# S5 parameters with both exponents on VectorE, and weight chunks in alternating order

## The chip, the cores and the metric

The kernel runs on one core of one Trainium2 chip. The metric is the device time of one execution in microseconds (us); lower is better. Engines are named TensorE (PE, its weight loads PEld), VectorE (DVE), ScalarE (ACT), GpSimd (POOL) and SyncE (SP, which issues most DMAs).

## The reference

One layer of a hybrid decoder trunk in float32, with 256 positions and a width of 2048:

```python
h = rmsnorm(x, norm1_w)
proj = h @ w_in                      # retention q,k,v,gate; mLSTM qk,v,o,gates; S5 input u
mix = concat[ silu(r_g) * groupnorm(retention(rope(q), rope(k), v)),     # 6 heads
              sigmoid(m_o) * groupnorm(mlstm(conv_silu(m_qk), m_v, gates)),  # 6 heads
              s5(u) ]                                                    # 32 groups, 64 states
x = x + mix @ w_out
h = rmsnorm(x, norm2_w)
x = x + (silu(gate) * val) @ w_down  # val, gate = split(conv3(h @ w_up)), 5632 each
return rmsnorm(x, final_norm_w)
```

The S5 part first turns its parameters, 32 groups of 64 complex states, into a discrete system:

```python
step = exp(log_step)[:, None]
mag = exp(ar * step)
abar_re, abar_im = mag * cos(ai * step), mag * sin(ai * step)
xr, xi = abar_re - 1.0, abar_im
den = ar * ar + ai * ai
fr, fi = (xr * ar + xi * ai) / den, (xi * ar - xr * ai) / den
```

It then scans the state over the 256 positions, reads it out, applies a gelu and a gated linear unit (GLU).

## The kernel before, in words

**Products.** Every float32 weight chunk of up to 1024 columns is loaded into a raw buffer (wr, 4 of them), cast by ScalarE to a high half (wh, 4), and VectorE writes the remainder as a low half (wl, 3). Activations are kept as a pair, high half beside low half, 256 columns each. `fm_tile` (line 521) computes one feature-major tile of 128 outputs: per chunk of eight blocks, `fm_part` (line 512) first runs eight matmuls of wh against the pair (512 columns, the high pass), then eight of wl against the high half (256 columns, the low pass), all into one PSUM bank. `chunk` (line 422) asks, at the start of each chunk, for loads five ahead, casts three ahead and remainders two ahead.

**Order of the work.** The S5 input product comes first (a loop over k at line 1200, with four or eight matmuls of each half per step), then 6 tiles for rotary queries and keys, 2 token-major tiles, 12 tiles of the mLSTM convolution, 6 token-major tiles, the output projection (partly as parts of chunks, with the GLU between, and 10 whole tiles), then 88 up tiles, 14 down tiles of 44 blocks (six chunks), and a token-major end.

**The planner.** Up to the MLP each engine's order is written out while the program is built. Every wrapped instruction (`V`, `S`, `G`, `mm`) advances a model clock of its engine by an estimated cost. Side work is a list of generators; `pump` (line 270) resumes one when the time that it yielded is due on VectorE's model clock and that clock isn't more than 0.35 us ahead of TensorE's. `hi_tasks` (evacuations, convolutions) go first, then `lo_tasks` in the order in which they were added: retention heads, gates, mLSTM heads, S5 parameters, S5 inputs, the four S5 groups, gelu. In the MLP a scheduler orders the engines by program order.

**S5 parameters.** `s5_params` (line 583) runs on POOL on tiles of 128 x 16: `exp_` (line 445) of the log step, the angle, its reduction and two series, `exp_` for the magnitude, three squarings of (cos, sin), the denominator with a power of -1, the two factors, and seven more squarings for the table of turns. POOL's `scalar_tensor_tensor` (line 221) is two POOL instructions. After POOL, VectorE multiplies the input matrices with the factors, TensorE transposes them, and VectorE doubles tables of cosine and sine out to 128 positions (line 686). `s5_inputs` and `s5_group` (lines 723 and 744) then take two PSUM banks and a pair of banks for each of the four groups, and VectorE does two pairs per group: products with the tables, scans, products back; 32 small matmuls read the state out.

**The start.** In the loop at line 1200, step j waits for its load of x and weights; ScalarE writes the high half of the activations, VectorE the low half (`xs[k][:, T:]`) and wl, and TensorE's matmuls read both.

Of the kernel before, what the change touches and what calls it, by code (L numbers as in the profile page):

```python
# [40 lines left out]
def kernel(ctx: ExitStack, tc: tile.TileContext, a: dict, out: bass.AP):  # L41
# [189 lines left out]
    def mm(o, lhsT, rhs, start, stop, par=1):  # L231
        fast = lhsT.dtype == F32R
        c = max(free(o) / 2400.0, 0.107) * (1 if fast else 4 if free(o) > 64 else 2) / par
        run("pe", c, [o], [lhsT, rhs])
        nc.tensor.matmul(o, lhsT=lhsT, rhs=rhs, start=start, stop=stop)  # L235
# [206 lines left out]
            "p (a b) -> p a b", a=shape[1]) if len(shape) > 2 else neg_half[:, :shape[1]], op=ALU.pow)  # L442
        return z

    def exp_(x, shape, lo=-87.0, hi=88.0):

        c, n, f, p = [tp(shape) for _ in range(4)]
        ni = tp(shape, I32)
        G.tensor_scalar(c, x, lo, hi, op0=MAX, op1=ALU.min)
        G.tensor_scalar(n, c, 1.4426950408889634, 12582912.0, op0=MUL, op1=ADD)  # L450
        G.tensor_scalar(n, n, 1.0, -12582912.0, op0=MUL, op1=ADD)
        G.scalar_tensor_tensor(f, n, -0.693145751953125, c, op0=MUL, op1=ADD)
        G.scalar_tensor_tensor(f, n, -1.42860682030941723e-6, f, op0=MUL, op1=ADD)

        G.tensor_scalar(ni, n, 127.0, 8388608.0, op0=ADD, op1=MUL)
        G.tensor_scalar(p, f, 1 / 5040, None, op0=MUL)
        for k in (1 / 720, 1 / 120, 1 / 24, 1 / 6, 0.5, 1.0):
            G.scalar_tensor_tensor(p, p, k, f, op0=ADD, op1=MUL)
        r = tn(shape)
        G.scalar_tensor_tensor(r, p, 1.0, ni.bitcast(F32), op0=ADD, op1=MUL)  # L460
        return r


# [45 lines left out]
        V.scalar_tensor_tensor(dst[:, T:], src, scale, dst[:, :T], op0=MUL, op1=SUB)  # L509


    def fm_part(ps, hl, ks, k0, acts, nk):

        h, l = hl
        ws = [(k, slice((k - k0) * 128, (k - k0 + 1) * 128)) for k in ks]
        for k, w in ws:
            mm(ps, lhsT=h[:, w], rhs=acts[k], start=(k == 0), stop=False)
        for k, w in ws:
            mm(ps[:, T:], lhsT=l[:, w], rhs=acts[k][:, :T], start=False, stop=(k == nk - 1))

    def fm_tile(first, acts, nk=KT):
        ps = acc_t()
        per = CH // 128
        for c in range(0, nk, per):
            fm_part(ps, chunk(first + c // per), range(c, min(c + per, nk)), c, acts, nk)
            if not auto[0]:
                pump()
        return ps
# [50 lines left out]
    def keep_up():  # L579

        return "dve", clk.pool

    def s5_params():
        sh = [128, 16]
        step_ = exp_(P("ls"), sh)
        yield keep_up()
        arg, th = tn(sh), tn(sh)
        G.tensor_tensor(arg, P("are"), step_, op=MUL)
        G.tensor_tensor(th, P("aim"), step_, op=MUL)

        c2 = math.floor((2.0 * math.pi - 6.28125) * 2.0 ** 20) / 2.0 ** 20
        c3 = 2.0 * math.pi - 6.28125 - c2
        k, ph, z, s, v, t = [tn(sh) for _ in range(6)]
# [9 lines left out]
        for cs, cc in ((1 / 120, -1 / 720), (-1 / 6, 1 / 24), (None, -0.5)):  # L603
# [4 lines left out]
        G.scalar_tensor_tensor(s, s, 1.0, ph, op0=ADD, op1=MUL)  # L608
        G.tensor_scalar(v, v, 1.0, 1.0, op0=MUL, op1=ADD)
        yield keep_up()  # L610
        mag = exp_(arg, sh)
        yield keep_up()

        def square(v, s):

            t, v2, s2_ = tp(sh), tn(sh), tn(sh)
            G.tensor_tensor(t, s, s, op=MUL)
            G.scalar_tensor_tensor(s2_, s, 2.0, v, op0=MUL, op1=MUL)
            G.tensor_scalar(v2, t, -2.0, 1.0, op0=MUL, op1=ADD)
            return v2, s2_  # L620

        for _ in range(3):
            v, s = square(v, s)
            yield keep_up()
        ar, ai = P("are"), P("aim")
        xr_, xi_, den, t1, t2, fr, fi = [tn(sh) for _ in range(7)]
        G.tensor_tensor(xr_, mag, v, op=MUL)
        G.tensor_tensor(xi_, mag, s, op=MUL)
        G.tensor_tensor(den, ar, ar, op=MUL)
        G.tensor_tensor(t1, ai, ai, op=MUL)  # L630
        G.tensor_tensor(den, den, t1, op=ADD)
        G.tensor_scalar(xr_, xr_, 1.0, -1.0, op0=MUL, op1=ADD)
        G.tensor_tensor(den, den, neg_one, op=ALU.pow)
        yield keep_up()
# [6 lines left out]
        turn = {1: (v, s)}  # L641
        for m in (1, 2, 4, 8, 16, 32, 64):
            turn[2 * m] = square(*turn[m])
            yield keep_up()

        yield "obj", lambda: "raws" in st
# [67 lines left out]
        st.update(cr=cr, nci=ci, ncr=ncr, ct=ct, sn=sn, er=turn[128][0], ei=turn[128][1], mag=mag)  # L714

    u_sb, y_sb = {}, {}

# [442 lines left out]
    add(ret_heads())  # L1160
    add(gates())
    add(ml_heads())
    add(s5_params())
    add(s5_inputs())
    for c in range(4):
        add(s5_group(c))
# [21 lines left out]
    clk.dve = clk.pool = 3.3  # L1188
    clk.act = 2.6
    sqs = []  # L1190

    def square():
# [4 lines left out]
            V.tensor_tensor(sqs[0], sqs[0], sq, op=ADD)  # L1197
        sqs.append(sq)

    for j, ks in enumerate(kts):  # L1200
        pump(until=max(last(raw[j].tensor.name), xat[ks[-1]]))
        if j > 1:
            highs_to(j)
        for k in ks:
            d = s2(F32R)
            S.activation(d[:, :T], xr[k // 2][:, (k % 2) * T:(k % 2 + 1) * T], AF.Copy, scale=P("n1", k))
            xs.append(d)
        if j > 1:
# [369 lines left out]
```

## Time and profile before

| what | us |
|---|---|
| median of 3 runs | 1159.4 (1158.87 to 1159.93) |
| profiled execution | 1158.52 |
| its span, first to last instruction | 1156.5 |
| TensorE busy | 1140.5 (99%) |
| VectorE busy | 870.0 (75%) |
| ScalarE busy | 625.0 (54%) |
| POOL busy | 95.0 (8%) |

Busy time is the union of an engine's instructions. Matmuls overlap in the records, so the pace of TensorE is read from the starts of successive matmuls, not from their durations. A row of the timeline merges neighbours of the same kind and gives the start of the first, the time from there to the end of the last, and their count; in brackets stand the idle time of the engine before it and what ended it.

### The profile page before, as it was taken

The numbers are of one execution on the slowest core, as the hardware profiler recorded it, in microseconds if no ns is written. First come the engines' busy times: TensorE is split into PE (matmuls) and PEld (weight loads), VectorE is DVE, ScalarE is ACT, GpSimd is POOL, SyncE is SP. The second block draws the span as 40 slices with busy tenths as digits, with TensorE's granted clock in tenths as the row PEclk, the third lists the DMA queues.
The fourth block names the chain that finished last, engine by engine and source line by source line (L and its number), as shares of the span: only waits on it lengthen the run. The fifth ranks groups of instructions, "written<-read, shape, count | busy, mean of one in ns | idle before, by whom it ended". The sixth has DMA issues, their size and how long they took to land.

```text
span 1156.5 us, 18142 instructions
## 1 busy us (share of the span) xinstructions
PE 1140.5 (99%) x6738; PEld 1013.0 (88%) x6738; DVE 870.0 (75%) x1478; ACT 625.0 (54%) x983; POOL 95.0 (8%) x228
## 2 busy tenths in 40 slices
PE   8999999999999999999999999999999999999997
PEld 7899888999778888888888888888888888888897
DVE  7778999989988678787877878778777655554554
ACT  7665555555546555555555555555555444444441
POOL 7936003010000000000000000000000000000000
PEclk9999999999999999999999999999999999999999
DMA  8667654455546656556555655656556666666662
GB/s 313 212 172 230 201 150 130 137 150 165 183 156 235 196 178 190 189 186 189 191 187 187 190 187 192 186 188 192 186 189 192 177 194 185 186 189 191 190 193 108
DMA packets 66905, 215.21 MB, mean 186 GB/s; under 512 B 7552, under 2 KB 9600, under 8 KB 66816
## 3 DMA queue, kind: packets, MB, share of 16 engines
q1 hardware_dynamic: 66672, 214.01, 59.5%
q8 instruction: 52, 0.85, 0.3%
q14 instruction: 37, 0.30, 0.1%
q10 hardware_dynamic: 144, 0.04, 0.0%
HBM read 211.92 MB, written 2.10 MB: 185 GB/s over the span
## 4 chain that ended last, share of the span: by engine, by line
PE 95%; DVE 3%; issue 1%; DMA 1%; SPq 0%; ACT 0%; POOL 0%; POOLq 0%; DVEq 0%; ACTq 0%
PE acc L235 90%; PE mis L235 3%; DVE s L183 2%; DVE wl L183 1%; PE wo L235 1%; PE u L235 1%; DMA s<-in_wu_dram 1%; PE mis L239 0%; SPq L1150 0%; SPq L385 0%; POOL t L218 0%; ACT wh L193 0%; ACT s L202 0%; DVE tp L183 0%; POOLq L1574 0%
## 5 line engine op out<-in xcount | busy, mean ns | idle before, releaser
L183 DVE TENSOR_TENSOR wl<-wr,wh 128x1024 fp32r<-128x1024 f32 (+3 forms) x409 | 473.4, 1158 | 247.8 <-PE acc L235 219.8
L193 ACT CAST wh<-wr 128x1024 fp32r<-128x1024 f32 (+3 forms) x409 | 406.4, 996 | 383.6 <-PE acc L235 338.0
L235 PE MATMUL acc<-s,wh 128*128 128x512 f32 x2372 | 602.5, 393 | 4.3 <-DVE s L183 4.3
L235 PEld LDWEIGHTS acc<-s,wh 128*128 128x128 f32 x2372 | 425.5, 189 | 81.3 <-DVE s L183 6.5
L235 PEld LDWEIGHTS acc<-s,wl 128*128 128x128 f32 x2372 | 327.4, 190 | 24.8
L235 PE MATMUL acc<-s,wl 128*128 128x256 f32 x2372 | 336.4, 282 | 0.0
L235 PE MATMUL acc<-wh,s 128*128 128x384 f32 (+2 forms) x632 | 159.4, 330 | 0.0
L183 DVE SCALAR_TENSOR_TENSOR s<-s,pp,s 128x255 f32<-128x255 f32 (+3 forms) x244 | 116.2, 479 | 3.9 <-ACT s L202 0.8
L183 DVE TENSOR_TENSOR s<-s,s 128x256 f32<-128x256 f32 (+4 forms) x242 | 111.2, 474 | 7.3 <-ACT s L202 3.2
L235 PEld LDWEIGHTS acc<-wh,s 128*128 128x128 f32 x632 | 112.2, 189 | 2.3 <-issue 1.1
L235 PE MATMUL acc<-wl,s 128*128 128x384 f32 (+2 forms) x316 | 103.0, 326 | 0.0
L202 ACT ACTIVATE s<-s,pp 128x256 f32<-128x256 f32 (+1 forms) x146 | 82.3, 567 | 16.4 <-DVE s L183 15.3
L218 POOL TENSOR_TENSOR t<-t,neg_half 128x2 f32<-128x2 f32 (+1 forms) x4 | 2.5, 632 | 892.2 <-DVE t L183 892.2
L202 ACT ACTIVATE s<-s 128x256 f32<-128x256 f32 (+2 forms) x106 | 45.5, 431 | 41.6 <-DVE s L183 41.4
L183 DVE TENSOR_TENSOR s<-acc,s 128x256 f32<-128x256 f32 x138 | 57.3, 417 | 3.5 <-PE acc L235 3.2
L235 PEld LDWEIGHTS acc<-wl,s 128*128 128x128 f32 x316 | 59.7, 189 | 0.0
L193 ACT COPY s<-acc 128x256 f32<-128x256 f32 x136 | 49.2, 364 | 12.7 <-PE acc L235 12.3
L235 PE MATMUL acc<-g,wh 128*128 128x512 f32 x196 | 50.0, 394 | 0.0
L183 DVE TENSOR_TENSOR s<-s,rbc 128x256 f32<-128x256 f32 x106 | 44.5, 423 | 3.8 <-ACT rbc L193 0.9
L235 PEld LDWEIGHTS acc<-g,wh 128*128 128x128 f32 x196 | 34.8, 188 | 6.2
L235 PE MATMUL mis<-s,s 128*32 128x256 f32 (+6 forms) x280 | 31.2, 352 | 0.6 <-DVE s L183 0.6
L235 PEld LDWEIGHTS acc<-g,wl 128*128 128x128 f32 x196 | 27.1, 189 | 2.3
(112 smaller groups left out, 487.2 us busy)
## 6 DMA issues: line engine op xcount, KB each, us to landing
wr<-in_wup_dram SPq DMA_DIRECT2D x176, 512.0 KB, 4.7
wr<-in_wdn_dram SPq DMA_DIRECT2D x70, 512.0 KB, 3.7
wr<-in_wtm_dram SPq DMA_DIRECT2D x56, 384.0 KB, 3.3
wr<-in_wfm_dram SPq DMA_DIRECT2D x36, 512.0 KB, 4.7
wr<-in_wout_dram SPq DMA_DIRECT2D x26, 512.0 KB, 4.0
wr<-in_wdt_dram SPq DMA_DIRECT2D x11, 512.0 KB, 3.8
s<-in_x_dram SPq DMA_DIRECT2D x14, 256.0 KB, 5.5
wr<-in_wdn_dram SPq DMA_DIRECT2D x14, 256.0 KB, 2.7
```

The costliest lines, as they stand in the source:

```text
L183: return real(o, *args, **kw)
L193: return nc.scalar.copy(o, i)
L202: return nc.scalar.activation(o, i, fn, **kw)
L218: return real(o, *args, **kw)
L235: nc.tensor.matmul(o, lhsT=lhsT, rhs=rhs, start=start, stop=stop)
```

## The change

`exp_` becomes a generator of steps that can run on POOL or on VectorE (with tiles of its own there). Both S5 exponents and the product between them, 29 instructions, go to VectorE: `fill` puts 3 of them ahead of each of the first two steps of the loop at line 1200 and 4 behind the activations' low halves, then 6 ahead of each later step until they are used up. The denominator and its power become POOL's first work on the parameters. `s5_params` waits until the step size has been issued, and, after three squarings, until the magnitude has. Sine and cosine lie side by side in one tile, and a squaring is three POOL instructions instead of four. The model clocks of VectorE and POOL start at 3.3 us before the S5 task is added instead of after. And `fm_tile` runs its odd chunks low pass first. The parts of the output projection, the GLU and the token-major tiles keep their order.

```diff
-    def exp_(x, shape, lo=-87.0, hi=88.0):
-        c, n, f, p = [tp(shape) for _ in range(4)]
-        ni = tp(shape, I32)
-        G.tensor_scalar(c, x, lo, hi, op0=MAX, op1=ALU.min)
...
+    def exp_steps(E, r, x, shape, lo=-87.0, hi=88.0):
+        c, n, f, p = [tn(shape) if E is V else tp(shape) for _ in range(4)]
+        ni = tn(shape, I32) if E is V else tp(shape, I32)
+        yield E.tensor_scalar(c, x, lo, hi, op0=MAX, op1=ALU.min)
...
+    def exp_(x, shape):
         r = tn(shape)
+        for _ in exp_steps(G, r, x, shape):
+            pass
         return r
...
-    def fm_part(ps, hl, ks, k0, acts, nk):
+    def fm_part(ps, hl, ks, k0, acts, nk, swap=False):
...
+        def highs():
+            for k, w in ws:
+                mm(ps, lhsT=h[:, w], rhs=acts[k], start=(k == 0), stop=(swap and k == nk - 1))
+        def lows():
+            for k, w in ws:
+                mm(ps[:, T:], lhsT=l[:, w], rhs=acts[k][:, :T], start=False, stop=(not swap and k == nk - 1))
+        for part in (lows, highs) if swap else (highs, lows):
+            part()
...
-            fm_part(ps, chunk(first + c // per), range(c, min(c + per, nk)), c, acts, nk)
+            fm_part(ps, chunk(first + c // per), range(c, min(c + per, nk)), c, acts, nk, swap=bool(c // per % 2))
...
+    def s5_exps():
+        step_, arg, mag = [tn(sh5) for _ in range(3)]
+        yield from exp_steps(V, step_, P("ls"), sh5)
+        st["step"] = step_
+        yield V.tensor_tensor(arg, P("are"), step_, op=MUL)
+        yield from exp_steps(V, mag, arg, sh5)
+        st["mag"] = mag
+    def s5_den():
...
+        G.tensor_tensor(den, den, neg_one, op=ALU.pow)
+        return den
-    def s5_params():
-        step_ = exp_(P("ls"), sh)
+    def s5_params(den):
+        yield "obj", lambda: "step" in st
...
-        mag = exp_(arg, sh)
...
+        def square(vs):
+            w, o = tp([128, 2, 16]), tn([128, 2, 16])
+            G.tensor_tensor(w, vs, vs[:, 1:2].to_broadcast([128, 2, 16]), op=MUL)
+            G.tensor_scalar(o[:, 0], w[:, 1], -2.0, 1.0, op0=MUL, op1=ADD)
+            G.tensor_scalar(o[:, 1], w[:, 0], 2.0, None, op0=MUL)
+            return o
...
+        yield "obj", lambda: "mag" in st
...
-    add(s5_params())
+    clk.dve = clk.pool = 3.3
+    add(s5_params(s5_den()))
...
+    exps = s5_exps()
+    def fill(n):
+        for _ in range(n):
+            next(exps, None)
     for j, ks in enumerate(kts):
+        fill(3 if j < 2 else 6)
         pump(until=max(last(raw[j].tensor.name), xat[ks[-1]]))
...
             V.scalar_tensor_tensor(xs[k][:, T:], xr[k // 2][:, (k % 2) * T:(k % 2 + 1) * T], P("n1", k),
                                    xs[k][:, :T], op0=MUL, op1=SUB)
+        fill(4 if j < 2 else 0)
         lows_to(j)
```

## Rows read from the trace of the kernel before

**Rows 1.** The page's summary line of the engines (busy us, share of the span, instructions) and the first line of the chain that ended last (share of the span by engine).

```profile
PE 1140.5 (99%) x6738; PEld 1013.0 (88%) x6738; DVE 870.0 (75%) x1478; ACT 625.0 (54%) x983; POOL 95.0 (8%) x228
...
PE 95%; DVE 3%; issue 1%; DMA 1%; SPq 0%; ACT 0%; POOL 0%; POOLq 0%; DVEq 0%; ACTq 0%
```

**Rows 2.** Busy time by stretch: from and to in us, length, then busy us and count of each engine, the granted TensorE clock, the busy share of the DMA engines, and GB/s.

```profile
3.10:14.00 10.90, 8.45 (x42) 7.24 (x41) 6.31 (x12) 7.07 (x13) 8.69 (x27) 1.00 0.97 341
30.00:120.00 90.00, 90.00 (x527) 82.93 (x526) 71.55 (x153) 54.77 (x94) 54.06 (x128) 1.00 0.67 209
120.00:225.00 105.00, 103.83 (x653) 93.67 (x651) 101.53 (x213) 57.09 (x98) 11.63 (x32) 1.00 0.53 155
300.00:345.00 45.00, 41.52 (x263) 31.86 (x263) 40.03 (x77) 24.44 (x41) 0.00 (x0) 1.00 0.46 149
345.00:1146.00 801.00, 800.78 (x4666) 707.68 (x4665) 561.21 (x841) 425.59 (x649) 1.24 (x2) 1.00 0.60 187
```

**Rows 3.** TensorE's timeline: the starts of two chunks of up tiles 70 chunks apart; inside one chunk the first and the sixth high matmul and the first low matmul; and two low matmuls of the token-major end, 51 matmuls of 256 columns apart.

```profile
699.39 2.00 PE L235 MATMUL acc<-s,wh 128*128 128x512 f32 x8
...
894.93 2.00 PE L235 MATMUL acc<-s,wh 128*128 128x512 f32 x8
...
704.98 0.40 PE L235 MATMUL acc<-s,wh 128*128 128x512 f32 x1
...
706.14 0.39 PE L235 MATMUL acc<-s,wh 128*128 128x512 f32 x1
...
706.82 0.28 PE L235 MATMUL acc<-s,wl 128*128 128x256 f32 x1
...
1117.00 0.28 PE L235 MATMUL acc<-wl,g 128*128 128x256 f32 x1
...
1123.12 0.28 PE L235 MATMUL acc<-wl,g 128*128 128x256 f32 x1
```

**Rows 4.** Timeline of VectorE and of TensorE: a remainder (wl) and the first matmul that reads it, in a conv tile and in an up tile.

```profile
123.86 1.22 DVE L183 TENSOR_TENSOR wl<-wr,wh 128x1024 fp32r<-128x1024 f32 x1
...
128.91 0.28 PE L235 MATMUL acc<-s,wl 128*128 128x256 f32 x1
...
702.39 1.23 DVE L183 TENSOR_TENSOR wl<-wr,wh 128x1024 fp32r<-128x1024 f32 x1 [0.77 <-PE acc L235]
...
709.62 0.28 PE L235 MATMUL acc<-s,wl 128*128 128x256 f32 x1
```

**Rows 5.** VectorE's timeline around 247 us: two small operations in the mLSTM heads, of which the second reads the first.

```profile
247.32 0.17 DVE L183 TENSOR_TENSOR t<-t,t 128x12 f32<-128x12 f32 x1
247.52 0.23 DVE L183 RECIPROCAL t<-t 128x12 f32<-128x12 f32 x1
```

**Rows 6.** VectorE's timeline at the start: its first operation, behind the landing of the parameters, and the low halves of the activations of two blocks.

```profile
3.17 0.17 DVE L183 TENSOR_SCALAR t<-pp 128x4 f32<-128x4 f32 x1 [3.17 <-DMA pp<-in_pp_dram]
...
13.51 0.87 DVE L183 SCALAR_TENSOR_TENSOR s<-s,pp,s 128x256 fp32r<-128x256 f32 x2
```

**Rows 7.** TensorE's timeline at the start: the two high passes that wait.

```profile
9.50 0.73 PE L235 MATMUL acc<-s,wh 128*128 128x512 f32 x2 [0.99 <-DVE s L183]
...
14.04 0.73 PE L235 MATMUL acc<-s,wh 128*128 128x512 f32 x2 [1.50 <-DVE s L183]
```

**Rows 8.** POOL's timeline: the two products behind the first exponent, the first instruction of the second exponent, the root of the first norm right behind its last, the denominator's power, and the first and the last of the 28 instructions of the seven squarings for the table of turns.

```profile
12.10 0.41 POOL L218 TENSOR_TENSOR t<-pp,t 128x16 f32<-128x16 f32 x2
...
28.70 1.14 POOL L218 TENSOR_SCALAR tp<-t 128x16 f32<-128x16 f32 x1
...
39.85 0.73 POOL L218 TENSOR_TENSOR t<-t,neg_half 128x2 f32<-128x2 f32 x1
...
47.70 3.09 POOL L218 TENSOR_TENSOR t<-t,neg_one 128x16 f32<-128x16 f32 x1
...
56.84 0.21 POOL L218 TENSOR_TENSOR tp<-t 128x16 f32<-128x16 f32 x1
...
66.15 0.93 POOL L218 TENSOR_SCALAR t<-tp 128x16 f32<-128x16 f32 x1
```

**Rows 9.** VectorE's timeline: the first products with the S5 factors, the first products of the first S5 group, and the first ones of the second pair of the last group.

```profile
73.25 1.28 DVE L183 TENSOR_TENSOR s<-s,t 128x512 f32<-128x512 f32 x2
...
143.50 1.28 DVE L183 TENSOR_TENSOR s<-mis,s 128x512 f32<-128x512 f32 x2
...
314.90 1.21 DVE L183 TENSOR_TENSOR s<-pj,s 128x1024 f32<-128x1024 f32 x1
```

**Rows 10.** TensorE's timeline from 300 us: the 32 read-out matmuls of the third S5 group, two waiting matmuls of the output projection, the 32 read-out matmuls of the last group in two rows, and a waiting matmul of the GLU.

```profile
300.44 1.93 PE L235 MATMUL mis<-s,s 128*32 128x256 f32 x32 [0.19 <-DVE s L183]
...
316.56 0.50 PE L235 MATMUL acc<-s,wh 128*128 128x512 f32 x1 [0.61 <-DVE s L183]
318.08 0.50 PE L235 MATMUL acc<-s,wh 128*128 128x512 f32 x1 [1.02 <-DVE s L183]
...
325.98 0.63 PE L235 MATMUL mis<-s,s 128*32 128x256 f32 x4
327.06 3.29 PE L235 MATMUL mis<-s,s 128*32 128x256 f32 x28 [0.45 <-DVE s L183]
...
332.27 0.51 PE L235 MATMUL mis<-s,wh 128*128 128x512 f32 x1 [1.03 <-DVE s L183]
```

**Rows 11.** VectorE's timeline inside POOL's power of 47.70 us.

```profile
49.29 1.75 DVE L183 TENSOR_TENSOR s<-s,s 128x256 f32<-128x256 f32 x5
```

More of the change, by code (lines that the diff above doesn't have):

```diff
@@ L443, in rsqrt_ @@
         return z
-    def exp_(x, shape, lo=-87.0, hi=88.0):
-        c, n, f, p = [tp(shape) for _ in range(4)]
-        ni = tp(shape, I32)
-        G.tensor_scalar(c, x, lo, hi, op0=MAX, op1=ALU.min)
[L450 to L456, printed above, removed]
+    def exp_steps(E, r, x, shape, lo=-87.0, hi=88.0):
+        c, n, f, p = [tn(shape) if E is V else tp(shape) for _ in range(4)]
+        ni = tn(shape, I32) if E is V else tp(shape, I32)
+        yield E.tensor_scalar(c, x, lo, hi, op0=MAX, op1=ALU.min)
+        yield E.tensor_scalar(n, c, 1.4426950408889634, 12582912.0, op0=MUL, op1=ADD)
+        yield E.tensor_scalar(n, n, 1.0, -12582912.0, op0=MUL, op1=ADD)
+        yield E.scalar_tensor_tensor(f, n, -0.693145751953125, c, op0=MUL, op1=ADD)
+        yield E.scalar_tensor_tensor(f, n, -1.42860682030941723e-6, f, op0=MUL, op1=ADD)
+        yield E.tensor_scalar(ni, n, 127.0, 8388608.0, op0=ADD, op1=MUL)
+        yield E.tensor_scalar(p, f, 1 / 5040, None, op0=MUL)
         for k in (1 / 720, 1 / 120, 1 / 24, 1 / 6, 0.5, 1.0):
-            G.scalar_tensor_tensor(p, p, k, f, op0=ADD, op1=MUL)
+            yield E.scalar_tensor_tensor(p, p, k, f, op0=ADD, op1=MUL)
+        yield E.scalar_tensor_tensor(r, p, 1.0, ni.bitcast(F32), op0=ADD, op1=MUL)
+    def exp_(x, shape):
         r = tn(shape)
-        G.scalar_tensor_tensor(r, p, 1.0, ni.bitcast(F32), op0=ADD, op1=MUL)
+        for _ in exp_steps(G, r, x, shape):
+            pass
         return r
@@ L509, in split_scaled @@
         V.scalar_tensor_tensor(dst[:, T:], src, scale, dst[:, :T], op0=MUL, op1=SUB)
-    def fm_part(ps, hl, ks, k0, acts, nk):
+    def fm_part(ps, hl, ks, k0, acts, nk, swap=False):
         h, l = hl
         ws = [(k, slice((k - k0) * 128, (k - k0 + 1) * 128)) for k in ks]
[L516 to L519, printed above, removed]
+        def highs():
[6 more added lines that the diff above has]
+            part()
     def fm_tile(first, acts, nk=KT):
@@ L581, in keep_up @@
         return "dve", clk.pool
-    def s5_params():
-        sh = [128, 16]
-        step_ = exp_(P("ls"), sh)
[L586 to L589, printed above, removed]
+    sh5 = [128, 16]
+    def s5_exps():
[6 more added lines that the diff above has]
+    def s5_den():
+        ar, ai = P("are"), P("aim")
+        den, t1 = [tn(sh5) for _ in range(2)]
+        G.tensor_tensor(den, ar, ar, op=MUL)
+        G.tensor_tensor(t1, ai, ai, op=MUL)
+        G.tensor_tensor(den, den, t1, op=ADD)
+        G.tensor_tensor(den, den, neg_one, op=ALU.pow)
+        return den
+    def s5_params(den):
+        sh = sh5
+        yield "obj", lambda: "step" in st
+        th = tn(sh)
+        G.tensor_tensor(th, P("aim"), st["step"], op=MUL)
         c2 = math.floor((2.0 * math.pi - 6.28125) * 2.0 ** 20) / 2.0 ** 20
         c3 = 2.0 * math.pi - 6.28125 - c2
-        k, ph, z, s, v, t = [tn(sh) for _ in range(6)]
+        k, ph, z, s, v = [tn(sh) for _ in range(5)]
         G.tensor_scalar(k, th, 1.0 / (2.0 * math.pi), 12582912.0, op0=MUL, op1=ADD)
@@ L607, in s5_params @@
             yield keep_up()
-        G.scalar_tensor_tensor(s, s, 1.0, ph, op0=ADD, op1=MUL)
-        G.tensor_scalar(v, v, 1.0, 1.0, op0=MUL, op1=ADD)
+        vs = tn([128, 2, 16])
+        G.scalar_tensor_tensor(vs[:, 1], s, 1.0, ph, op0=ADD, op1=MUL)
+        G.tensor_scalar(vs[:, 0], v, 1.0, 1.0, op0=MUL, op1=ADD)
         yield keep_up()
-        mag = exp_(arg, sh)
[L612 to L620, printed above, removed]
+        def square(vs):
[4 more added lines that the diff above has]
+            return o
         for _ in range(3):
-            v, s = square(v, s)
+            vs = square(vs)
             yield keep_up()
+        v, s = vs[:, 0], vs[:, 1]
+        yield "obj", lambda: "mag" in st
+        mag = st["mag"]
         ar, ai = P("are"), P("aim")
-        xr_, xi_, den, t1, t2, fr, fi = [tn(sh) for _ in range(7)]
+        xr_, xi_, t1, t2, fr, fi = [tn(sh) for _ in range(6)]
         G.tensor_tensor(xr_, mag, v, op=MUL)
         G.tensor_tensor(xi_, mag, s, op=MUL)
-        G.tensor_tensor(den, ar, ar, op=MUL)
-        G.tensor_tensor(t1, ai, ai, op=MUL)
-        G.tensor_tensor(den, den, t1, op=ADD)
         G.tensor_scalar(xr_, xr_, 1.0, -1.0, op0=MUL, op1=ADD)
-        G.tensor_tensor(den, den, neg_one, op=ALU.pow)
-        yield keep_up()
         for o, x0, x1_, op in ((fr, xr_, xi_, ADD), (fi, xi_, xr_, SUB)):
@@ L640, in s5_params @@
             yield keep_up()
-        turn = {1: (v, s)}
+        turn = {}
         for m in (1, 2, 4, 8, 16, 32, 64):
-            turn[2 * m] = square(*turn[m])
+            vs = square(vs)
+            turn[2 * m] = vs[:, 0], vs[:, 1]
             yield keep_up()
@@ L713, in s5_params @@
                 yield from double(ct[c], sn[c], slice(4 * c, 4 * c + 4), 4, m)
-        st.update(cr=cr, nci=ci, ncr=ncr, ct=ct, sn=sn, er=turn[128][0], ei=turn[128][1], mag=mag)
+        st.update(cr=cr, nci=ci, ncr=ncr, ct=ct, sn=sn, er=turn[128][0], ei=turn[128][1])
     u_sb, y_sb = {}, {}
@@ L1187 @@
     ups += [pair[:, :512], pair[:, 512:]]
-    clk.dve = clk.pool = 3.3
     clk.act = 2.6
```

## The prediction, made before the changed kernel was run

> **What bounds the kernel now.** I read the engine summary first, then the chain that ended last, then a table of stretches. TensorE is busy 1140.5 of 1156.5 us, and it is 95% of the chain [rows 1]. So only two things pay: less time per matmul, and fewer holes in TensorE's row. The table of stretches shows the holes [rows 2]: 2.45 us between 3.1 and 14.0 us, 1.17 us between 120 and 225 us, 3.48 us between 300 and 345 us, none between 30 and 120 us, and 0.22 us in the 801 us of the gated MLP. The granted clock is 1.00, the level of 2.4 GHz, in all of them. In the same table VectorE idles 18.45 us between 30 and 120 us and only 3.47 us between 120 and 225 us.
>
> **Part 1: the chunks alternate.** A chunk of a feature-major tile is eight matmuls of 512 columns (high pass), then eight of 256 (low pass). From 699.39 to 894.93 us there are 70 chunks, 2.7934 us each [rows 3]. Inside one, the first five high matmuls take 1.16 us (704.98 to 706.14), 0.232 us each, the last three 0.68 us (706.14 to 706.82), 0.2267 us each. So after a low pass TensorE needs five matmuls to come to its pace, and they cost 1.16 - 5 x 0.2267 = 0.0265 us. Matmuls of 256 columns hold 0.120 us over a long run: 51 of them from 1117.00 to 1123.12 us [rows 3]. A chunk at both steady paces would be 8 x 0.2267 + 8 x 0.120 = 2.7736 us, so one return to the high pass, with the small credit on entering the low pass, costs 2.7934 - 2.7736 = 0.0198 us.
>
> With odd chunks low pass first, the order is high, low, low, high, and the next tile begins high: every second return goes. That is one for each of the 28 feature-major tiles before the MLP (6 + 12 + 10) and the 88 up tiles, and three for each of the 14 down tiles of six chunks: 158 x 0.0198 = **3.1 us less**. The ends are 0 (the loss doubles after a doubled low pass) and 4.2 (158 x 0.0265, the credit stays). I take 3.1, since the low pace is flat after its second matmul and the high pace after its fifth. A loss is excluded: it would need a pace worse than the steady ones that the rows show.
>
> The price is that an odd chunk's low half (wl) is due a high pass, 1.84 us, earlier. In the MLP wl ends at 702.39 + 1.23 = 703.62 us and is first read at 709.62 us: 6.0 us to spare. The tightest odd chunk of the conv tiles ends at 125.08 us and is read at 128.91 us: 3.8 us [rows 4]. Both cover it. An odd chunk's wh is released a low pass later; ScalarE casts three chunks ahead of TensorE, which hides that 0.95 us; without this cover each odd chunk would cost it. No DMA moves.
>
> **Part 2: both exponents on VectorE at the start.** 29 small operations (14, one product, 14), each reading the one before. The trace has no such chain, so I bound the step from the nearest rows: dependent operations on 12 columns begin 0.20 us apart (247.32 to 247.52), and one lasts 0.17 us [rows 5]; a 4-column one during POOL's work lasts 0.17 us too [rows 6]. So 29 x 0.20 = 5.8 us. Between 3.1 and 14.0 us VectorE is busy 6.31 of 10.9 us [rows 2], so 4.6 us are free, but split into pieces by waits for ScalarE's casts. TensorE waits here: 0.99 us before 9.50 and 1.50 us before 14.04 [rows 7], both for a low half of the activations, and the second is written from 13.51 us [rows 6]. I walked the new order, 3 + 4 operations in each of the first two steps, then 6, 6 and 3. Step one and two stay covered (their matmuls wait for the casts). The 9.50 becomes about 10.5 and the 14.04 about 14.9. **0.9 us more**, on the path because TensorE has no hole afterwards until 180 us. The ends are 0 (steps of 0.16 us fit the free time) and 2 (steps of 0.24 us).
>
> **Part 3: what POOL is rid of.** The second exponent held POOL from 28.70 to 39.9 us, 11.2 us [rows 8]. The phase began at 12.10 us, behind the first exponent; now it can start when VectorE has done its first fourteen operations, near 7.5 us: 4.6 us sooner. The denominator's power takes 3.09 us [rows 8] and moves to POOL's first microseconds after the parameters land, where it ends before 7.5 us. Seven squarings of four instructions took 10.2 us (56.84 to 67.08) [rows 8], 0.37 us an instruction; ten squarings lose one each, 3.7 us, less for the double width of another: I take 3. In all POOL ends 4.6 + 11.2 + 3.1 + 3 = 22 us sooner, at about 45 us. Behind the new wait for the step size on POOL's queue stands only S5 work and the first norm's root, which waited behind the second exponent before (39.85) [rows 8].
>
> None of this is on TensorE's path by itself. VectorE began S5's products at 73.25 us and the first group at 143.50 us [rows 9]; it was then full, so groups ran late, and the last one's products (314.90) stood in front of work that TensorE waited for. With the tables some 22 us sooner, VectorE does them in its idle time before 120 us, and the groups move up by what is recovered: I take half of the 18.45 us, about 9. What is late at the end: TensorE waits 1.02 us before 318.08; the last group's 32 read-out matmuls take from 325.98 to 330.35, 4.37 us, where the third group's took 1.93 us, so 2.4 us are lost; 1.03 us go before 332.27, and about 0.4 of the 0.61 us before 316.56 [rows 10]. Together 4.9 us, the upper end; 0 is the lower. The last group's second pair starts at 314.90 us [rows 9] and its read-out ends 15 us later, so nine microseconds free most but not all of it: **3.0 us less**. What is late next are the retention and mLSTM heads' transposes, which wait for the last gate tile.
>
> **Sum.** 0.9 - 3.1 - 3.0 = -5.2 us. The profiled execution took 1158.52 us (span 1156.5, 2.0 us around it), 0.9 us under the median of 1159.4. So 1153.3 on its scale, **1154.2 us** on the median's. About 0.2% (2.3 us) can be told from no change.
>
> **The rivals.** First, the order of the passes is worth nothing: a matmul costs its columns and a constant. TensorE then keeps 2.79 us a chunk and the time is 1157.3 us. Against it, equal matmuls take 0.232 and 0.2267 us by their place [rows 3]. The Trainium skill, TensorE: Matmul & The Clock Gate, section Back-to-back issue gap, has this rule, the spacing being columns over 2.4 GHz plus 2.5 ns; the trace disagrees, with 0.2267 us and more for 512 columns.
>
> Second, S5 gains nothing: the groups' places are set by PSUM banks and by the planner, which runs heads first, or POOL does not end sooner. 0.9 - 3.1 gives 1157.2 us. For it: between 300 and 345 us VectorE idles 5.0 us while TensorE waits for it [rows 2], so its load alone does not set the order.
>
> Third, POOL's power stops VectorE at the start. The price is its 3.09 us [rows 8], so 1157.3 us. Against it, VectorE did five two-input products in 1.75 us from 49.29 us, inside the power of 47.70 to 50.79 us [rows 8, 11]. The Trainium skill, SBUF — State Buffer, section Who interferes with whom, says that such operations and a POOL read lock each other out for a whole instruction; here the trace disagrees.
>
> Fourth, slower: between 102 and 171 us, where the conv tiles leave VectorE 3.47 us in 105 [rows 2], S5 groups pulled forward fill its queue ahead of wl. It decides once VectorE falls behind by the 3.8 us margin [rows 4] less the 1.84 us: then each of the 12 odd chunks waits. At half a microsecond each, 6 us, with no gain from S5: 1159.4 + 0.9 - 3.1 + 6 = 1163.2 us.
>
> **Chances.** Forecast 0.55, first rival 0.12, second 0.18, third 0.04, fourth 0.11. The first three rivals lie at the bound of 1157.1 us, so under half of their 0.34 counts as faster: 0.52 + 0.15 = 0.67 faster, 0.21 the same, 0.12 slower. The range goes from 1150.8 (4.9 from S5, 4.2 from the order, 0.5 at the start) to 1158.4, over the three rivals with a worse start; slower is left out.
>
> **What would show it.** Right: two chunks in the MLP take 5.567 us, not 5.587; the second stall at the start ends near 14.9 us; POOL's parameters end near 45 us; the last read-out takes about 2 us. Wrong: high matmuls at 0.232 us in the second half of the run of sixteen, a first S5 product that still comes at 70 us, or holes with wl as releaser between 102 and 171 us.

## The result, and the profile after

The changed kernel takes **1148.74 us** (1148.46 to 1148.82, four runs) against 1159.13 us (1158.62 to 1159.93, four runs) before: a ratio of 0.9909, interval 0.9892 to 0.9926. That is 10.4 us less, where 5.2 were forecast, and below the range. The two profiled executions, from which the rows come, lie 9.7 us apart (1158.52 and 1148.82).

The profiled execution after: the engine summary and the chain, for [rows 1].

```profile
PE 1134.9 (99%) x6738; PEld 1012.7 (88%) x6738; DVE 867.7 (76%) x1507; ACT 625.9 (55%) x983; POOL 76.5 (7%) x171
...
PE 94%; POOL 3%; DVE 2%; issue 1%; DMA 0%; ACT 0%; POOLq 0%; DVEq 0%; SPq 0%
```

The stretches of [rows 2] after (the same columns).

```profile
3.10:14.00 10.90, 8.66 (x42) 6.64 (x41) 10.10 (x41) 7.05 (x13) 9.28 (x19) 1.00 0.97 342
30.00:120.00 90.00, 89.77 (x527) 82.37 (x526) 80.95 (x181) 54.08 (x92) 31.50 (x80) 1.00 0.67 209
120.00:225.00 105.00, 104.32 (x661) 93.62 (x661) 102.53 (x212) 58.19 (x100) 13.30 (x31) 1.00 0.51 153
300.00:345.00 45.00, 45.00 (x280) 38.69 (x279) 33.97 (x59) 26.30 (x42) 0.00 (x0) 1.00 0.63 210
```

VectorE works 80.95 of the 90 us from 30 to 120 us, up from 71.55. Between 300 and 345 us the roles have changed: TensorE has no hole, VectorE idles 11 us. The 3% of POOL in the chain are its work on the S5 parameters up to 36 us, behind which the first norm's root stands on its queue (35.94 us, before 39.85); TensorE waits 0.22 us for that norm.

POOL's timeline after, for [rows 8]: the denominator's power, the first work on the step size (0.17 us behind VectorE), the last factors, and the end of the last squaring.

```profile
4.05 3.00 POOL L218 TENSOR_TENSOR t<-t,neg_one 128x16 f32<-128x16 f32 x1
7.22 0.60 POOL L218 TENSOR_TENSOR t<-pp,t 128x16 f32<-128x16 f32 x1 [0.17 <-DVE t L183]
...
31.14 1.45 POOL L218 TENSOR_TENSOR t<-t,t 128x16 f32<-128x16 f32 x2
...
42.11 1.44 POOL L218 TENSOR_SCALAR t<-tp 128x16 f32<-128x16 f32 x2
```

VectorE's S5 work after, for [rows 9].

```profile
43.97 1.29 DVE L183 TENSOR_TENSOR s<-s,t 128x512 f32<-128x512 f32 x2
...
104.33 1.27 DVE L183 TENSOR_TENSOR s<-mis,s 128x512 f32<-128x512 f32 x2
...
290.10 1.22 DVE L183 TENSOR_TENSOR s<-pj,s 128x1024 f32<-128x1024 f32 x1
```

POOL's tables end at 43.5 us instead of 67. The first products come 29 us sooner, the first group 39 us, the last group's second pair 25 us.

TensorE after, for [rows 10]: the start of the output projection, the last group's read-out, and the matmul behind the GLU.

```profile
302.36 0.39 PE L235 MATMUL acc<-s,wh 128*128 128x512 f32 x1
...
314.25 1.93 PE L235 MATMUL mis<-s,s 128*32 128x256 f32 x32
...
330.22 0.40 PE L235 MATMUL wo<-s,wh 128*128 128x512 f32 x1
```

The same first and last matmul before.

```profile
302.50 0.48 PE L235 MATMUL acc<-s,wh 128*128 128x512 f32 x1
...
337.30 0.40 PE L235 MATMUL wo<-s,wh 128*128 128x512 f32 x1
```

Nearly the same work (182 matmuls; before, 184, with two small transposes more) takes 27.9 us instead of 34.8. The waits of [rows 10], one of 0.16 us more and the longer read-out account for some 5.2 us of the 6.9 that are gone. Of the other 1.7, the two transposes are 0.3; the rest is time lost around each wait that no idle column shows. The matmul ahead of 316.56 us, for one, starts at 315.55 us; the next would have started 0.23 us later and starts 1.01 us later, but since the record of the first lasts 0.40 us the row marks 0.61 us of these 0.78.

TensorE in the up tiles after, for [rows 3]: one period of two chunks, between two high passes 35 periods apart.

```profile
689.35 0.86 PE L235 MATMUL acc<-s,wh 128*128 128x512 f32 x3
...
706.05 3.82 PE L235 MATMUL acc<-s,wh 128*128 128x512 f32 x16
709.70 2.08 PE L235 MATMUL acc<-s,wl 128*128 128x256 f32 x16
...
884.18 1.09 PE L235 MATMUL acc<-s,wh 128*128 128x512 f32 x4
```

Two chunks take 194.83 / 35 = 5.567 us. The start, for [rows 7]: TensorE's three waits.

```profile
10.01 0.73 PE L235 MATMUL acc<-s,wh 128*128 128x512 f32 x2 [1.48 <-DVE s L183]
12.05 0.74 PE L235 MATMUL acc<-s,wh 128*128 128x512 f32 x2 [0.38 <-DVE s L183]
14.11 0.73 PE L235 MATMUL acc<-s,wh 128*128 128x512 f32 x2 [0.37 <-DVE s L183]
```

And for [rows 6], VectorE's low half for the last of them.

```profile
13.57 0.88 DVE L183 SCALAR_TENSOR_TENSOR s<-s,pp,s 128x256 fp32r<-128x256 f32 x2
```

Where the time went, from the start of each part's first matmul, with the two halves of the change run apart (below):

| first matmul of | before | after | order alone | S5 alone |
|---|---|---|---|---|
| rotary tiles | 30.95 | 31.02 | 31.25 | 31.08 |
| ten whole output tiles | 351.52 | 344.45 | 351.55 | 344.91 |
| up tiles | 407.39 | 400.15 | 407.25 | 400.77 |
| down tiles | 900.51 | 891.59 | 898.71 | 893.90 |
| token-major end | 1116.17 | 1106.44 | 1113.55 | 1109.56 |
| end of the span | 1156.47 | 1146.88 | 1153.84 | 1149.86 |

### The profile page after: what moved, and what is told of

Its sections match the earlier page's. It is cut to its first block, busy times and chain, and to the rows that moved or that the text cites. A ratio compares the mean times of both kernels' runs of the same rounds, so it can differ in the third digit from the quotient of the medians.

```text
span 1146.9 us, 18221 instructions
## 1 busy us (share of the span) xinstructions
PE 1134.9 (99%) x6738; PEld 1012.7 (88%) x6738; DVE 867.7 (76%) x1507; ACT 625.9 (55%) x983; POOL 76.5 (7%) x171
## 4 chain that ended last, share of the span: by engine, by line
PE 94%; POOL 3%; DVE 2%; issue 1%; DMA 0%; ACT 0%; POOLq 0%; DVEq 0%; SPq 0%
PE acc L235 90%; PE mis L235 3%; POOL t L218 2%; DVE s L183 1%; PE wo L235 1%; POOL tp L218 1%; PE mis L239 0%; DMA wr<-in_wu_dram 0%; DVE wl L183 0%; DVE t L183 0%; ACT wh L193 0%; POOLq L1611 0%; ACT s L202 0%; DVE tp L183 0%; SPq L1179 0%
## 5 line engine op out<-in xcount | busy, mean ns | idle before, releaser
L183 DVE TENSOR_TENSOR wl<-wr,wh 128x1024 fp32r<-128x1024 f32 (+3 forms) x409 | 462.3, 1155 | 159.2 <-PE acc L235 101.8
L235 PE MATMUL acc<-s,wh 128*128 128x512 f32 x2372 | 576.1, 392 | 2.3 <-DVE s L183 2.2
L235 PEld LDWEIGHTS acc<-s,wh 128*128 128x128 f32 x2372 | 433.7, 188 | 86.8 <-DVE s L183 3.4
L235 PEld LDWEIGHTS acc<-s,wl 128*128 128x128 f32 x2372 | 308.6, 191 | 14.4 <-DVE wl L183 0.5
L235 PE MATMUL acc<-s,wl 128*128 128x256 f32 x2372 | 315.5, 283 | 0.1
L183 DVE TENSOR_TENSOR s<-s,s 128x256 f32<-128x256 f32 (+6 forms) x242 | 111.7, 475 | 45.5 <-ACT s L202 40.9
```

The source lines that it names most:

```text
L183: return real(o, *args, **kw)
```

## The experiments

In the diffs, + and - stand against the kernel that the text names. "Before" in these comparisons is 1159.2 to 1160.0 us.

**The two halves apart.** On the kernel before, `fm_tile` of the changed kernel; on the changed kernel, the other way round:

```diff
+            fm_part(ps, chunk(...), range(...), c, acts, nk, swap=bool(c // per % 2))
```

> The kernel before with the alternating chunks alone (S5 untouched). Theory A, the parts add: each of the 158 removed returns to the high pass is worth 0.0198 us, so 1159.1 - 3.1 = 1156.0 us; the 88 up tiles shorten by 1.7 us, the 14 down tiles by 0.8 us, and the holes between 300 and 345 us stay as before. Rival B, the order also shifts the planner's clocks so far that part of the S5 gain comes with it: under 1154 us, with fewer holes between 300 and 345 us. Rival C, the order is worth nothing: 1159.1 us.

> The changed kernel with every chunk high pass first again (the S5 part alone). Theory A, the parts add: the S5 part carries the whole difference up to the first up tile, 7 us, and the order the rest: 1148.7 + 3.1 = 1151.8 us, and TensorE has no hole between 300 and 345 us. Rival B, the two parts need each other (the order decides where the planner puts the groups): 1153.5 us or more, with holes between 300 and 345 us.

Order alone: 1156.82 us, ratio 0.9976 (0.9966 to 0.9985). S5 alone: 1152.03 us, ratio 0.9939 (0.9927 to 0.9952). By the table, the order gives 1.66 us in the up tiles, 0.8 in the down tiles and 0.2 in the ten output tiles. Ahead of those it seems to give nothing (351.55 against 351.52), but that execution began its rotary tiles 0.30 us later: from there on it is 320.30 instead of 320.57 us, where 18 tiles x 0.0198 would be 0.36. S5 gives all of its 6.6 us before the ten output tiles. On top of the S5 part the order is worth 1152.0 - 1148.7 = 3.3 us by the medians, alone 2.4. The intervals, 1 to 2 us to either side, don't separate these two, and by the table, from the rotary tiles on, both are 2.9 us. Rivals B and C of the first, and B of the second, are out.

**The price of a return.** On the changed kernel, `fm_part` runs four high, four low, four high, four low:

```diff
-        for part in (lows, highs) if swap else (highs, lows):
-            part()
+        for part in (ws[:4], ws[4:]):
...
```

> The changed kernel with every feature-major chunk in four passes of four blocks (high, low, high, low) and no alternation: two returns to the high pass per chunk instead of one per two chunks. Theory A, each return costs 0.0167 to 0.0198 us by its place in the run: 460 returns more than in the changed kernel (84 before the MLP, 264 in the up tiles, 112 in the down tiles), so 7.7 to 9.1 us more: 1156.4 to 1157.8 us. Rival C, the order is worth nothing (the time was S5's alone): 1148.7 us.

1155.0 us, ratio to the kernel before 0.9960 (0.9947 to 0.9972): 6.3 us more than the changed kernel. The up tiles take 495.30 us instead of 491.44, 0.0146 us for each of 264 returns; the down tiles 216.08 instead of 214.85, 0.011 us for each of 112. The price is real, but the time lies under the range of theory A: a return costs less in runs of four, which the timeline shows.

```profile
700.25 1.09 PE L235 MATMUL acc<-s,wh 128*128 128x512 f32 x4
701.18 0.63 PE L235 MATMUL acc<-s,wl 128*128 128x256 f32 x4
701.65 0.63 PE L235 MATMUL acc<-s,wh 128*128 128x512 f32 x2
```

Four high ones take 0.93 us (4 x 0.2267 would be 0.907), four low ones 0.47 (4 x 0.120 would be 0.48). So four high ones lose 0.02 us, where the first five of a run lose 0.0265 in all: a run of four ends before its fifth slow step. The credit in the low pass, 0.01 us at this resolution, is about that of a run of eight.

**The start.** On the kernel before, the 29 operations on VectorE as well, unused:

```diff
+        fill(3 if j < 2 else 6)
...
+        fill(4 if j < 2 else 0)
```

> The kernel before, with the 29 small operations also done on VectorE at the start, by the same filling, and their results left unused; POOL still computes both exponents. It prices the start alone. The prediction's step: the third and the fifth step of the loop slip, 1159.1 + 0.9 = 1160.0 us. Theory A: the fifth step's cast waits for its load until 11.2 us in both kernels, so the slip is caught up there and only some 0.1 us is left: 1159.2 us, with TensorE's last hole at the start ending near 14.1 us.

1162.41 us, ratio 1.0027 (1.0018 to 1.0035), which neither expectation held. But the start is not where it went: the rotary tiles begin at 31.31 us (before: 30.95; order alone, with nothing added there: 31.25). The other 2.5 us appear from 170 us on, at new waits, the longest this one:

```profile
234.44 0.44 PE L235 MATMUL mis<-s,t 38*128 38x256 f32 x2 [1.44 <-DVE t L183]
```

The 29 operations advance the planner's model clock, and it wrote another order of the heads and groups for 300 us. That raised a rival that the prediction had only in passing: that the order drawn decides. The next runs set the time of the tables against it.

**The time of the tables.** On the changed kernel, unused squarings hold POOL back (twenty and ten of them):

```diff
+        for _ in range(20):
+            G.tensor_tensor(dw, vs, vs[:, 1:2].to_broadcast([128, 2, 16]), op=MUL)
+            G.tensor_scalar(do[:, 0], dw[:, 1], -2.0, 1.0, op0=MUL, op1=ADD)
+            G.tensor_scalar(do[:, 1], dw[:, 0], 2.0, None, op0=MUL)
```

> The changed kernel with 60 more small POOL instructions (20 unused squarings) behind the first three squarings, which hold the S5 tables back by some 24 us, to about where they were ready before; the exponents stay on VectorE, the chunks alternate. Theory A, the time of the tables carries the S5 gain: the groups go back to late places, TensorE waits for VectorE between 300 and 345 us again, and the time is about 1148.7 + 7 = 1155.7 us. Rival B, the gain comes from the planner's new order and the emptier POOL as such, not from when the tables are ready: under 1151 us. Rival D, it is the load on VectorE in the rest that matters and any place of the groups before 300 us does: between, 1151 to 1154 us.

> The changed kernel with 30 more small POOL instructions (10 unused squarings) behind the first three squarings: the tables some 13 us later than in the changed kernel, near 57 us. Theory A, the time of the tables carries the S5 gain, in proportion: half of the 7 us is gone, about 1152 us. Theory A2, it carries it with a threshold, since the last read-out of the changed kernel comes 14 us before that of the kernel before and only some 7 us of that are used: 1149 to 1150 us. Rival B, any rearrangement by the planner may cost or give several us whatever the tables' time: over 1156 us or scattered.

1168.62 us, ratio 1.0083 (1.0067 to 1.0098), and 1159.69 us, ratio 1.0002 (0.9993 to 1.0012). The first lies above all three of its theories, the second above theory A and its threshold, where rival B had it. And the first is 9 us slower than the kernel before with its products at nearly the same time (76.47 and 73.25 us). The largest wait of TensorE with twenty squarings, and POOL's timeline before it:

```profile
315.59 1.34 PE L239 MATMUL mis<-ident,s 128*128 128x128 f32 x4 [7.79 <-DVE s L183]
```

```profile
301.71 2.30 POOL L218 TENSOR_TENSOR t<-tp,neg_half 128x12 f32<-128x12 f32 x1
```

Here the order puts the last heads' norm, with POOL's power in it, at 302 us; in the kernels before and after it runs near 254 us. TensorE waits for those heads' transposes.

Some of the 9 us is TensorE's clock: it works some 7 us at a granted clock of 0.50 there, an estimate of 3.6 us lost (last section).

Then parts of the change undone. Both exponents back on POOL; and, in another kernel, the denominator behind the squarings and squarings of four instructions:

```diff
+        st["step"] = exp_(P("ls"), sh)
...
+        mag = st["mag"] = exp_(arg, sh)
```

> The changed kernel with both exponents back on POOL, the denominator still first, sine and cosine still side by side, the chunks alternating, and nothing added at the start of VectorE. Tables near 61 us. Theory A, by the time of the tables: 1148.7 + 7 x 17/24 = 1153.7 us. Theory A2 (threshold): 1151 to 1153 us. Rival B, the planner's order decides: not between 1149 and 1157 us, or below the half dose.

> The changed kernel with the denominator and its power back behind the squarings, and the squarings of four instructions; the exponents stay on VectorE, the chunks alternate. Tables near 51 us, 7 us later than in the changed kernel. Theory A, in proportion: 1148.7 + 2 = 1150.8 us. Theory A2 (threshold): 1148.7 us. Rival B: over 1153 us.

1159.71 us, ratio 0.9999 (0.9990 to 1.0008); and 1153.65 us, ratio 0.9948 (0.9933 to 0.9963). VectorE's first products come at 74.02 and 55.06 us. The direction is theory A's, and both times lie where rival B had them. But the first is no partial dose: POOL's tables end at 66.3 us there, not near 61, against 67 before. Its profiled execution (1161.04 us) also lost 1.7 us at the start, where the granted clock was 0.50, the level of 1.2 GHz, after TensorE had waited 1.92 us before 14.19 us:

```profile
64.98 1.34 POOL L218 TENSOR_SCALAR t<-tp 128x16 f32<-128x16 f32 x2
```

```profile
14.50:17.50 3.00, 3.00 (x10) 2.50 (x9) 2.75 (x6) 3.00 (x7) 2.56 (x6) 0.50 1.04 414
```

And tables earlier in the kernel before, with no work added on VectorE:

```diff
-        mag = exp_(arg, sh)
+        mag = step_
```

> The kernel before with the second exponent left out (the magnitude is the step size, so the result is not the reference's): POOL is 11.2 us sooner at the tables, near 56 us, and VectorE has nothing more to do. Theory A, 0.35 to 0.7 us of time for each us of the tables: 1151.7 to 1155.5 us, with fewer holes between 300 and 345 us. Theory A2 (threshold, or half the movement is enough): 1152 to 1153 us. Rival B, the planner's order decides: not between 1151 and 1156 us.

1155.62 us, ratio 0.9969 (0.9959 to 0.9980): about 4 us for VectorE's first products at 62.13 instead of 73.25 us. Here theory A holds, at its edge (1155.5): earlier tables pay with nothing added on VectorE, though the order is drawn anew here too.

**The order drawn.** On the kernel before, the S5 work ahead of the heads in the list; and, in another kernel, only the model clock advanced, no instruction changed:

```diff
+            clk.dve += left.pop(0)
```

> The kernel before with its list of side work reordered alone: S5 parameters, inputs and groups ahead of the retention heads, the gates and the mLSTM heads; parameters on POOL as before, so tables at 67 us. If the place of the groups in VectorE's order is what counts (theory A, by way of that order), the groups come earlier without earlier tables and part of the 7 us comes: 1153 to 1156 us. If the heads then come late instead, it gains nothing or loses: 1159 us or more, with TensorE waiting for transposes of the heads. Rival B, the tables' time as such: 1159 us, the groups' places unchanged.

> The kernel before with no instruction added or removed: only the planner's model clock of VectorE is advanced at the start by what it books for the 29 operations (3.5 us in all), so that it draws another order of the same work. Rival B, the order that the planner happens to draw is worth some us by itself: the time differs from 1159.4 us by over 1.5 us, either way (the 29 unused operations cost 3 us, of which at most 0.4 us at the start). Theory A, only the tables' time counts: 1159.4 us within 1 us, since POOL's work and the tables' time are untouched.

1189.89 us, ratio 1.0260 (1.0245 to 1.0276): the first group stays where it was (143.04 us against 143.50 before), so it wasn't the list that made it late; the later groups come sooner, and now the heads are last, which costs one wait of over 10 us:

```profile
338.74 0.45 PE L239 MATMUL mis<-ident,s 128*128 128x128 f32 x1 [10.39 <-DVE s L183]
```

The model clock alone: 1166.03 us, ratio 1.0062 (1.0049 to 1.0075). The same instructions and tables in another order cost 6 us. So one pair of kernels cannot say what earlier tables are worth. Four more runs draw the order anew in both programs, each with alternating chunks, by the planner's lead of VectorE over TensorE:

```diff
-    SLACK = 0.35
+    SLACK = 0.2
```

> The kernel before with alternating chunks (1156.8 us), and the planner's lead of VectorE over TensorE set to 0.2 us instead of 0.35: the same work in another order, tables at 67 us. Theory A (the tables' time sets the level, the order drawn scatters around it): within 1156 to 1166 us, and above the kernel with the S5 part at the same lead. Rival B (the order drawn is all): the two families overlap.

> The kernel before with alternating chunks, and a lead of 0.45 us. Theory A: 1156 to 1166 us, and above the kernel with the S5 part at the same lead by 4 to 10 us. Rival B: the two families overlap.

> The changed kernel (tables at 43.5 us) with a lead of 0.2 us. Theory A: 1147.7 to 1152 us; with the tables early VectorE has time in hand, so the order drawn scatters less than with late tables. Rival B: as far from 1148.7 us as the kernels with late tables are from 1156.8 us, 1155 us among them.

> The changed kernel with a lead of 0.45 us. Theory A: 1147.7 to 1152 us. Rival B: as far from 1148.7 us as the kernels with late tables are from 1156.8 us, 1155 us among them.

| lead | S5 as before | S5 changed | less |
|---|---|---|---|
| 0.20 | 1162.55 | 1151.67 | 10.9 |
| 0.35 | 1156.82 | 1148.74 | 8.1 |
| 0.45 | 1166.31 | 1151.27 | 15.0 |

(Ratios to the kernel before: 1.0027, 1.0065, 0.9933 and 0.9931, each interval within 0.0020 of them.) The families do not overlap. Late tables scatter by 9.5 us, early ones by 2.9: theory A in the direction of every pair, if over its bound in the last, and rival B's scatter, but for late tables above all. Three draws each can say no more. The lead of 0.35 us is the best draw of the late family, so the 7 us measured are less than earlier tables bring in the other two pairs.

Much of the late family's scatter is TensorE's clock. In the profiled executions with late tables the granted clock is 0.50 in two stretches with a lead of 0.20 (the first two rows, columns as in [rows 2]), in three with 0.45 (the others), and in none with 0.35.

```profile
304.00:310.50 6.50, 3.37 (x10) 2.65 (x11) 5.08 (x11) 5.19 (x10) 0.00 (x0) 0.50 0.00 0
328.00:331.00 3.00, 3.00 (x10) 2.50 (x9) 1.95 (x3) 1.04 (x1) 0.00 (x0) 0.50 0.64 150
...
14.50:17.50 3.00, 3.00 (x10) 2.50 (x9) 2.80 (x5) 3.00 (x7) 2.53 (x7) 0.50 1.03 406
308.00:314.50 6.50, 2.66 (x19) 1.29 (x22) 5.59 (x26) 0.34 (x1) 4.68 (x6) 0.50 0.19 61
318.50:324.50 6.00, 4.93 (x14) 3.93 (x15) 3.41 (x6) 2.97 (x6) 0.00 (x0) 0.50 0.06 14
```

TensorE works 6.4 and 10.6 us in them, of which half is lost, an estimate of 3.2 and 5.3 us. With early tables the clock is 1.00 from 14 to 1141 us in all three. Taken off the profiled executions, that leaves 7.2, 8.1 and 11.4 us between the pairs at 0.35, 0.20 and 0.45. With the model clock advanced alone TensorE works some 3 us at 0.50, with S5 first some 29, with ten squarings none: waits come with the draw, and the granted clock adds to some of them.

**A still earlier start of S5.** On the changed kernel, the seven squarings as a task of their own, so that the products wait for the factors alone:

```diff
+        def turns(vs):
+            for m in (1, 2, 4, 8, 16, 32, 64):
+                vs = square(vs)
...
+        lo_tasks.insert(0, [turns(vs), ("dve", 0.0)])
```

> The changed kernel with the seven squarings for the table of turns as a task of their own, so that VectorE's products with the S5 factors and TensorE's transposes of the input matrices wait only for the factors (near 32 us on POOL) and no longer for the squarings (43.5 us). Theory A2 (threshold): TensorE has no hole left between 300 and 345 us and only 1.0 us of holes between 30 and 300 us, so at most that comes: 1147.7 to 1148.7 us. Theory A (in proportion, 0.6 to 0.8 us of time for each us of the tables): 1142 us. Rival B, the planner's new order costs what it wins or more: 1149 to 1153 us.

1151.17 us, ratio 0.9926 (0.9914 to 0.9938): 2.4 us above the changed kernel, though the first products come at 34.24 us. Rival B. No version run here beats the changed kernel.

**What all of them share.** From 14 us to the ten whole output tiles: the kernel before, the changed one, order alone, no second exponent, the denominator and squarings back, ten squarings, the model clock alone, twenty squarings (columns as in [rows 2]).

```profile
14.00:351.52 337.52, 332.58 (x2038) 298.92 (x2039) 301.48 (x618) 194.75 (x328) 84.00 (x192) 1.00 0.58 181
```

```profile
14.00:344.45 330.45, 329.32 (x2038) 298.67 (x2039) 300.88 (x619) 195.95 (x328) 64.89 (x143) 1.00 0.59 185
```

```profile
14.00:351.55 337.55, 332.29 (x2038) 298.85 (x2039) 301.80 (x619) 195.10 (x328) 84.30 (x192) 1.00 0.59 181
```

```profile
14.00:348.63 334.63, 330.98 (x2039) 298.87 (x2039) 301.50 (x619) 195.84 (x329) 72.08 (x169) 1.00 0.59 182
```

```profile
14.00:349.04 335.04, 331.78 (x2038) 298.31 (x2039) 301.04 (x619) 195.70 (x328) 73.61 (x157) 1.00 0.59 182
```

```profile
14.00:355.25 341.25, 334.07 (x2038) 298.49 (x2039) 301.27 (x619) 198.95 (x330) 85.27 (x172) 1.00 0.58 178
```

```profile
14.00:358.69 344.69, 334.99 (x2039) 300.44 (x2039) 303.21 (x619) 197.90 (x330) 90.88 (x192) 1.00 0.57 177
```

```profile
14.00:364.38 350.38, 334.00 (x2039) 301.13 (x2040) 303.49 (x619) 197.66 (x330) 94.62 (x203) 0.99 0.57 174
```

VectorE's work is 301 to 303 us in every one, so the kernels differ in when it works, not in how much: it idles 36.0 us before and 29.6 after. That its load bounds the stretch is not shown, and the idle time that it recovers early doesn't set the time by itself: with ten squarings it works 76.67 us between 30 and 120 us, 5 more than before, and the stretch is 3.7 us longer. TensorE's side bounds the gain. After the change it is busy 329.32 of 330.45 us and idles 1.1, against 4.9 before. So of 337.52 us some 8.2 were there to be won, and 7.1 came: little is left.

```profile
30.00:120.00 90.00, 89.79 (x525) 82.40 (x524) 76.67 (x167) 54.61 (x93) 43.96 (x109) 1.00 0.67 208
```

## Why the prediction was wrong

**The failed step: the size of the S5 term**, "nine microseconds free most but not all of it: 3.0 us less", and the 4.9 given as its upper end. Measured alone it is 7.1 us. The steps ahead of it held: POOL ended at 43.5 us (about 45 was said), and VectorE recovered 9.4 us of idle time before 120 us (9 was said). Two things went wrong behind them. The recovered time was taken as the groups' movement; they moved by 25 to 39 us, since VectorE's order is redrawn and not shifted, and so everything that was late between 302 and 337 us came off, not three fifths of it. And the gain was counted in waits that a row marks: 4.9 us, where the same stretch of work shrank by 6.9 (34.8 to 27.9 us). The marked waits and the read-out hold only some 5.2 of these; the time lost around the waits and two transposes held the rest. That VectorE recovered nearly what was forecast is no support for the step from there to the time: other orders that recovered some of it were slower than the kernel before. How much of the 7.1 us is this draw's luck stays open: where both kernels alternate, the S5 part brings 8.1, 10.9 and 15.0 us by the lead.

**The order** was forecast at 3.1 us: 2.4 alone, 3.3 on top of the S5 part, 2.9 by the table in both, and 5.567 us for two chunks, as forecast. Right. The first rival is out: the sixteen high matmuls of the changed kernel take 3.65 us (706.05 to 709.70), 16 x 0.2267 us and one loss of 0.0265, so equal matmuls take a pace that depends on their place here too. The Trainium skill (TensorE: Matmul & The Clock Gate, section Back-to-back issue gap) gives columns over 2.4 GHz plus 2.5 ns as the gap of an isolated matmul; this trace disagrees, with 0.2267 us and more for 512 columns.

**The start** was forecast at 0.9 us and can't be told from nothing: the rotary tiles begin at 31.02 us after and 31.08 with S5 alone, at 30.95 before and 31.25 with the order alone. The low half of the fifth step begins at 13.57 us instead of 13.51 [rows 6], TensorE's last wait ends at 14.11 instead of 14.04. The step of 0.20 us was right (two operations behind the first took 0.38 us), VectorE fills the idle pieces (10.10 busy of 10.90 us), and the third step's wait grew by 0.5 us (it ends at 10.01 us), half of what was said. The walk let that slip run on to the fifth step. It does not, since ScalarE's cast there begins at the same time, 11.24 us before and 11.27 after:

```profile
11.27 1.05 ACT L193 CAST wh<-s 128x1024 fp32r<-128x1024 f32 x1 [1.03 <-PE u L235]
```

The cast waits for its load, not for the matmul named: the last piece of that load lands at 11.14 us before and 11.17 after, and with both exponents on POOL the row of the same cast names it.

```profile
11.43 1.05 ACT L193 CAST wh<-s 128x1024 fp32r<-128x1024 f32 x1 [1.59 <-DMA s<-in_wu_dram]
```

**The other rivals.** S5 gains nothing: out. POOL's power stops VectorE: out, since the remainder of 512 columns inside the power of 4.05 us takes 0.69 us, as it did before.

```profile
4.82 0.69 DVE L183 TENSOR_TENSOR wl<-wr,wh 128x512 fp32r<-128x512 f32 x1
```

Groups ahead of wl: not in this draw, where no hole before the MLP has wl as releaser; but with a lead of 0.2 us the changed program has just that, at an odd chunk's low pass:

```profile
172.37 0.86 PE L235 MATMUL acc<-s,wl 128*128 128x256 f32 x5 [1.31 <-DVE wl L183]
```

For that rival the prediction read VectorE's 3.47 us of idle time as that of 102 to 171 us; its row is of 120 to 225 us, and in 102 to 171 us VectorE idles 5.5 of 69 us.

What stays open is why the planner's order at one setting is better than at the next; the runs show only how far it scatters.

## What to carry to other kernels

Where the main engine waits for a side engine, price the stretch by what its work takes at the paces that the same trace shows elsewhere (here 1.84 us for eight high matmuls, 1.93 us for a read-out), and don't add up the waits that rows mark: here they and the read-out held 5.2 of 6.9 us. Ask what the side engine could not start for want of: here a small chain of parameters on a slow engine, 24 us too long, cost 7 us at a place 270 us later. And where a planner writes the order, draw it several times in both versions before crediting a change, and look at the granted clock of each: with work late three draws lay 9.5 us apart, of which the clock is an estimate of up to 5.3, with work early 2.9.

## What the hardware showed unexpectedly

A long wait costs twice. With S5 as before and a lead of 0.45 us, TensorE waits 6.57 us before 311.84 and 3.91 before 319.55. The rows of the waits, of the matmuls behind the second, and the granted clock there (in the rows of stretches the last three columns are the clock, the DMA share and GB/s):

```profile
311.84 3.79 PE L235 MATMUL mis<-s,s 128*32 128x256 f32 x28 [6.57 <-DVE s L183]
319.55 1.34 PE L239 MATMUL mis<-ident,s 128*128 128x128 f32 x4 [3.91 <-DVE s L183]
320.54 3.76 PE L235 MATMUL acc<-s,wh 128*128 128x512 f32 x8
324.10 1.50 PE L235 MATMUL acc<-s,wl 128*128 128x256 f32 x8
```

```profile
321.00:325.00 4.00, 4.00 (x13) 3.23 (x13) 2.04 (x3) 1.33 (x2) 0.00 (x0) 0.51 0.18 58
325.00:330.00 5.00, 5.00 (x30) 4.40 (x30) 3.78 (x5) 2.46 (x3) 0.00 (x0) 1.00 0.50 163
```

It is at 0.50, the level of 1.2 GHz, until about 325 us, and eight high matmuls take 3.56 us from start to start of what follows, instead of 1.84. The Trainium skill (TensorE: Matmul & The Clock Gate, section What's actually happening) says that the throttled state is the default and activity releases it; this trace agrees. The waits of the kernel before, 1.03 us at most at that place, left the clock at 1.00. The clock also fell inside the wait of 7.79 us with twenty squarings, which ends at 315.59 us, and was at 1.00 again some 4 us behind it.
